# Row maxima of two heads made together on two halves of TensorE's rows, and the output projection written in half rows

## The chip, the cores and the metric

The kernel runs on one core of a Trainium2 chip. The time is the device time of one execution, in microseconds, and the figure compared is the median over runs. The engines named below are TensorE (PE, with its weight loads PEld), VectorE (DVE), ScalarE (ACT), GpSimd (POOL) and SyncE (SP), whose queue issues nearly all DMAs. Matmul results land in PSUM, which has eight banks of 128 x 512 float32.

## The reference, cut to what matters

One layer of a hybrid encoder over two sequences, 2048 and 512 tokens of width 1024. A projection feeds four groups of mixers (A to D), whose outputs are gated, put side by side and projected back. Group C is attention with 4 heads of width 64 and 2 key heads, so that two heads share their keys:

```
def one_block(q_blk):
    s = jnp.einsum("bqkgd,bskd->bkgqs", q_blk, k, preferred_element_type=jnp.float32) * scale
    p = jax.nn.softmax(s, axis=-1)
    return jnp.einsum("bkgqs,bskd->bqkgd", p.astype(v.dtype), v)
...
mix = jnp.concatenate([y_a, y_b, y_c, y_d], axis=-1)
return x + mix @ w_out
```

The softmax subtracts a row's maximum from its scores before the exponential; any number near the maximum serves, since it cancels in the quotient.

## The kernel before, in words

Tokens go in five blocks of 512: blocks 0 to 3 are the long sequence, block 4 the short one. Float32 values are carried as two float16 parts, high and low, so that products are made of two or three float16 matmuls.

The phases overlap. Phase 1 makes the columns of B and A, phase 2 makes three passes for the other columns, group B (a gated recurrence, `deltanet`) runs beside them, and `phase3` holds attention and the output projection. All instructions pass through a scheduler that writes, ahead of the run, one fixed order for each engine, by priorities and a model of the time. Attention has a priority offset of 2000000, the recurrence 3000000, the last pass of gates (lines 607 to 769) 1000000, and the output projection -2000000. On an engine the order is then fixed: what stands behind a waiting instruction waits too.

`phase3` works through a list of (sequence, block, head). One step of `attn` takes 128 keys against the block's 512 queries:

- scores `sp` (lines 909 and 910) are two matmuls: `KA` (128 rows, the keys' high part above their low part) against `qa` (the queries' high part twice), then `KB` (64 rows of the keys' high part and a row of ones) against `qb` (the queries' low part and, in its 65th row, minus the row maximum);
- `e` = exp of the scores (ACT, line 912); `p` is its high part (ACT, line 915) and its rest (line 916, DVE, at every fourth step POOL);
- twelve small matmuls add `p` times the values to `O` (line 921).

A head of blocks 0 to 3 has 16 steps, a head of block 4 has 4: 272 steps in all. The maxima for the next head come from the generator `row_max`, one unit per step: one matmul `mp` (line 884) of 128 queries against 512 keys, over all 128 rows, so high part times both key parts, and one reduction (DVE, line 886). When a head's units are through, the negated maxima are turned by four small matmuls `mr` (line 892) and put into `qb` (line 894). The first head's maxima are made ahead of all steps. `load_q` fetches a head's `qa` and `qb` (lines 870 and 871), at the start of its maxima.

Beside each step `pump` places one unit of the waiting work: first what is left of the gates (`rest`, from step 28), then the output projection of the blocks in turn (`outproj`). A unit of it is three matmuls of line 958; 24 matmuls make one group `op` of 128 tokens x 512 columns, which DVE scales and adds to `xr` (line 962) into `y`. `xr` and `y` hold whole rows of 1024. What is left when the steps are over runs behind them.

PSUM banks have the names a0, a1, b0, b1, c, d0, d1, e. `BANKS` gives a list for each use, which is gone through in turn: S for scores, M for the maxima (and for two transposes at a block's end), X for `op`. A digit behind the letter marks another list: S0 and M0 in block 0, S2 and M2 in block 4, X1 and X2 for the output projection of blocks 3 and 4.

Of the kernel before, what the change touches and what calls it, by code (L numbers as in the profile page):

```python
# [7 lines left out]
F32 = mybir.dt.float32  # L8
# [29 lines left out]
URG = 4000000  # L38
MAGIC = float(0x5F3759DF)
# [5 lines left out]
class Trunk:  # L45
    BANKS = dict(A=("a0", "a1"), B=("b0", "b1"), C=("c",), D=("d0", "d1"), E=("e",),
                 S=("a0", "a1", "b1"), O=("b0",), M=("c", "d1", "d0"), X=("e",), P=("a0", "a1", "e"),
                 AA=("a0", "a1", "d0"), F=("a0", "a1"), NA=("a0", "a1"), B0=("b0", "b1", "c", "e"), S0=("a0", "a1"), M0=("c", "b1"), X0=("e",),
                 M2=("c", "d1"), X1=("e", "d0"), X2=("e", "d0", "a0", "a1", "b1", "c"), S2=("a0", "a1", "b1"))
# [38 lines left out]
    def split3(self, parts, x, V=None):  # L88
        """x (float32, destroyed) as the sum of three float16"""
        V = V or self.nc.vector  # L90
        for i, p in enumerate(parts):
            V.tensor_copy(p, x)
            if i < 2:
                V.tensor_tensor(x, x, p, op=ALU.subtract)
# [35 lines left out]
    def mm_fm2(self, ps, w, x, mid=None):  # L130
        """two columns at once, so that each part of x is done with early"""
# [45 lines left out]
    def late_consts(self, p):  # L177
        """p: the pool of those that phase 1 alone reads"""
# [21 lines left out]
    def phase1(self):  # L200
# [3 lines left out]
        with ExitStack() as ctx:  # L204
# [31 lines left out]
            def load_x(b):  # L236
# [11 lines left out]
                if b == 0:  # L248
                    # the squares of the transposed tiles, added up over the features by the tensor engine
# [314 lines left out]
    def phase2(self, names, ep, shared, stop=None):  # L564
        """one pass over the blocks before stop for the columns in names; shared: the tags of ep for the gates.
        Returns what yields after each part of the products of a block"""
# [42 lines left out]
        def norm_sums(sq, h):  # L609
            # sq: [128, 512] squares; 1 / rms of each of the h heads, in three parts, heads on partitions  # L610
# [26 lines left out]
        def pool_block(b, f):  # L637
# [3 lines left out]
            def add(o, i, r, a, c, w):  # L641
                # o[t] = i[t - a] + i[t + c] for t in [-w, 512 + w)
# [25 lines left out]
        def pool_ready(b, f):  # L668
            """a block's part of d_x has come: what it completes"""
# [12 lines left out]
        def store_qk(dst, s):  # L682
            # s: [64 half + 32 head + j or 32 head + j, hi and lo, half, tokens]
# [9 lines left out]
        def rope_q(a, c, cs):  # L693
            # the turn leaves the norm as it is, which comes after it
# [81 lines left out]
        def chain(sq, h, finish):  # L776
            """the norm of the heads, each step in its turn"""
# [70 lines left out]
    def phase3(self, kp, ap, wp, ep, e5, rest, post):  # L848
        """SBUF pools: kp of the keys, ap of the steps, wp of the output's weights, ep and e5 of its products;
        rest: what is left of the other columns"""  # L850
        tc, nc, I = self.tc, self.nc, self.I
        V, A, G, PE, NB = nc.vector, nc.scalar, nc.gpsimd, nc.tensor, self.NB
        if True:
# [12 lines left out]
            def load_q(b, h):  # L866
                qa = ap.tile([128, 512], F16, tag="qa", name="qa")
                qb = ap.tile([65, 512], F16, tag="qb", name="qb")
# [5 lines left out]
            def row_max(seq, b, h):  # L874
                """yields after each part of the maxima of a block and head; then they stand in qb"""
                s0, n, KA, KB, vt = seq
                q = qs[b, h] = load_q(b, h)
                qa, qb = q
                nsc = n // 512
                mm = ap.tile([128, 4, nsc], F32, tag="mm", name="mm")  # L880
                for qt in range(4):
                    for sc in range(nsc):
                        mp = self.bank("M" + w0(b), [128, 512], "mp")
                        PE.matmul(mp, qa[:, qt * 128:qt * 128 + 128], KA[h // 2][:, sc * 512:sc * 512 + 512],  # L884
                                  start=True, stop=True)
# [590 lines left out]
```

## Time and profile before

| | |
|---|---|
| median of 3 runs | 1581.37 us (1578.85 to 1585.43) |
| span of the profiled execution | 1580.7 us |
| busy, PE / PEld / DVE / ACT / POOL | 1470.4 / 836.2 / 1176.9 / 815.7 / 545.7 us |
| instructions | 34819 |
| DMA | 269.66 MB, mean 171 GB/s |

The profile is one execution of the program. Its span is all that it gives as that execution's own time, and it lies 0.7 us under the median. A row of a group of instructions gives line, engine, operation, tiles out and in, shape, count, busy time, mean duration in ns, and the idle time of its engine just ahead of it with what ended it. Shapes of matmuls are rows\*columns of the array in use, then the moving operand. Matmuls overlap each other, so the busy time of PE is not a sum of durations.

### The profile page before, as it was taken

How to read it: one execution, taken by the hardware profiler on the slowest of the kernel's cores; microseconds unless marked ns; L12 is line 12 of the kernel's file. 1: busy time of each engine (PE TensorE's matmuls, PEld its weight loads, DVE VectorE, ACT ScalarE, POOL GpSimd, SP SyncE). 2: the span in 40 equal slices, each digit the busy share in tenths (PEclk: the TensorE clock that was granted, in tenths of full speed). 3: DMA queues.
4: the chain of work that ended last, by engine and by line, in shares of the span. 5: the costliest groups of instructions: out<-in, count | busy, mean ns of one | idle time of the engine just before them, and what ended most of it. 6: DMA issues, size and time to landing. Idle time of an engine off the chain costs nothing. (4 is left out here: it accounts for less than half of the span.)

```text
span 1580.7 us, 34819 instructions
## 1 busy us (share of the span) xinstructions
PE 1470.4 (93%) x13420; PEld 836.2 (53%) x13420; DVE 1176.9 (74%) x2265; ACT 815.7 (52%) x1695; POOL 545.7 (35%) x646
## 2 busy tenths in 40 slices
PE   6999999998899799999989989989899999999898
PEld 3456555543455464566545545555455555555443
DVE  6348569966969779886887768999987787786621
ACT  5245444445455755556346414566666675576500
POOL 3220220044747646344353545464222121121100
PEclk9999999998999799989899999999999999999999
DMA  8845544456565867747578897554411411413333
GB/s 252 282 167 172 187 135 124 147 192 189 159 192 194 263 180 246 209 154 214 181 225 262 286 286 241 174 175 136 161 56 60 147 37 60 164 33 124 124 127 107
DMA packets 250832, 269.66 MB, mean 171 GB/s; under 512 B 95785, under 2 KB 176681, under 8 KB 250025
## 3 DMA queue, kind: packets, MB, share of 16 engines
q1 hardware_dynamic: 250264, 267.36, 54.0%
q8 instruction: 105, 1.72, 0.5%
q14 instruction: 63, 0.51, 0.1%
q0 software_dynamic: 400, 0.07, 0.1%
HBM read 175.66 MB, written 91.77 MB: 169 GB/s over the span
## 5 line engine op out<-in xcount | busy, mean ns | idle before, releaser
L127 PEld LDWEIGHTS <-w 128*128 128x128 f16 x2280 | 222.6, 101 | 283.0 <-issue 55.7
L127 PE MATMUL accz<-xs,w 128*128 128x512 f16 x960 | 239.1, 398 | 7.9 <-DMA xs<-xs 3.9
L958 PE MATMUL op<-wo,mx 128*128 128x512 f16 x960 | 225.8, 380 | 2.6 <-DMA mx<-mix 1.9
L886 DVE TENSOR_REDUCE mm<-mp 128x1 f32<-128x512 f32 x272 | 177.5, 681 | 50.4 <-PE mp L884 49.8
L912 ACT ACTIVATE e<-sp 128x512 f32<-128x512 f32 x272 | 153.1, 597 | 89.6 <-PE sp L910 84.3
L916 POOL TENSOR_TENSOR p<-e,p 128x512 f16<-128x512 f32 x68 | 87.4, 1286 | 312.1 <-ACT p L915 262.8
L916 DVE TENSOR_TENSOR p<-e,p 128x512 f16<-128x512 f32 x204 | 171.1, 856 | 22.3 <-ACT p L915 22.2
L127 PE MATMUL acc<-xs,w 128*128 128x512 f16 x720 | 162.8, 383 | 3.8 <-POOL xs L291 1.5
L915 ACT ACTIVATE p<-e 128x512 f16<-128x512 f32 x272 | 160.7, 633 | 1.0
L921 PEld LDWEIGHTS <-p 128*128 128x128 f16 x3264 | 129.1, 97 | 56.6 <-DVE p L916 12.9
L921 PE MATMUL O<-vt,p 128*128 128x65 f16 (+1 forms) x3264 | 143.3, 193 | 9.1 <-DVE p L916 7.7
L958 PEld LDWEIGHTS <-mx 128*128 128x128 f16 x960 | 91.0, 98 | 104.5 <-DMA mx<-mix 2.0
L884 PE MATMUL mp<-ka,qa 128*128 128x512 f16 x272 | 93.3, 380 | 11.4 <-DVE mm L886 3.8
L306 DVE SCALAR_TENSOR_TENSOR cv<-raw,convw,cv 128x512 f32<-128x512 f32 x120 | 87.7, 751 | 21.2 <-POOL raw L382 20.6
L909 PE MATMUL sp<-qa,ka 128*128 128x512 f16 x272 | 102.5, 380 | 1.0 <-ACT e L912 0.6
L910 PE MATMUL sp<-qb,kb 65*128 65x512 f16 x272 | 98.3, 380 | 1.4 <-ACT qb L894 1.2
L1257 POOL TENSOR_TENSOR kd<-kv,kds 128x512 f16<-128x512 f32 x40 | 45.2, 1131 | 146.7 <-PE up L1294 120.1
L127 PE MATMUL accq<-xs,w 128*128 128x512 f16 x360 | 89.2, 394 | 3.1 <-ACT rawp L834 1.0
L400 PE MATMUL acct<-wtm,xs 128*128 128x400 f16 x480 | 85.5, 337 | 1.8 <-ACT ba L408 0.9
L291 POOL TENSOR_TENSOR xs<-xt,xs 128x512 f16<-128x512 f32 x36 | 49.1, 1387 | 75.9 <-ACT xs L288 75.6
L1131 POOL TENSOR_TENSOR at<-dt,at 128x512 f16<-128x512 f32 x40 | 53.7, 1342 | 57.3 <-ACT at L1130 47.5
L962 DVE SCALAR_TENSOR_TENSOR y<-op,xr 128x512 f32<-128x512 f32 x40 | 27.4, 685 | 55.0 <-PE op L958 54.6
(316 smaller groups left out, 2628.8 us busy)
## 6 DMA issues: line engine op xcount, KB each, us to landing
xs<-xs SPq DMA_DIRECT2D x120, 256.0 KB
kx<-kx SPq DMA_DIRECT2D x80, 256.0 KB
at<-at SPq DMA_DIRECT2D x80, 256.0 KB
tt<-tt SPq DMA_DIRECT2D x80, 256.0 KB
xt<-in_xT SPq DMA_DIRECT2D x40, 256.0 KB
xs<-xs SPq DMA_DIRECT2D x5, 2048.0 KB
kv<-kv SPq DMA_DIRECT2D x40, 256.0 KB
mix<-mixs SPq DMA_DIRECT2D x40, 256.0 KB
```

What stands on the lines that cost most here:

```text
L127: mm = self.nc.tensor.matmul(ps, w[:, a, k, :], xk, start=k + i == 0, stop=k == 7 and i == 2)
L306: V.scalar_tensor_tensor(cv, raw[:, ct, i:i + 512], self.convw[:, ct, i:i + 1], cv, op0=ALU.mult, op1=ALU.add)
L400: PE.matmul(acc[:, 0:400], xs[:, a, k, tt * 128:(tt + 1) * 128], w[:, c, k, :], start=n == 0, stop=n == 23)
L884: PE.matmul(mp, qa[:, qt * 128:qt * 128 + 128], KA[h // 2][:, sc * 512:sc * 512 + 512], start=True, stop=True)
L886: V.tensor_reduce(mm[:, qt, sc:sc + 1], mp, axis=AX.X, op=ALU.max)
L909: PE.matmul(sp, KA[kv][:, c], qa, start=True, stop=False)
L910: PE.matmul(sp, KB[kv][:, c], qb, start=False, stop=True)
L912: A.activation(e, sp, AF.Exp)
L915: A.activation(p[:, 0], e, AF.Copy)
L916: (G if st % E8 == 1 else V).tensor_tensor(p[:, 1], e, p[:, 0], op=ALU.subtract)
L921: mm = PE.matmul(O[:, qt, 0:z - a], p[:, w, q], v[:, a:z], start=st == 0 and qt == 0 and i == 0, stop=st == nst - 1 and i == 2, skip_group ...
L958: PE.matmul(op, mix[k][:, a, tt * 128:tt * 128 + 128], wo[k][:, c, n * 512:n * 512 + 512], start=i + j == 0, stop=i == 7 and j == 2)
```

## The change

- Scores get two banks instead of three in all blocks; the maxima get four (c, d1, d0, b1) in blocks 1 to 4. The output projection of block 3 gets one bank (e) instead of two.
- `row_max` now makes the maxima of heads h and h+1 together. Each unit is two matmuls of 64 rows: head h on rows 0 to 63 against `KB`, head h+1 on rows 64 to 127 against `KA`. Only high parts are multiplied. In block 0 one unit of both heads is made at a time, elsewhere two units (four matmuls), then their reductions. The generator is asked for the next part at every fourth step over the two heads, and runs to its end behind the second head.
- The four `mr` matmuls and the copy into `qb` follow for the two heads one after the other.
- `KA` has its parts the other way up, the low part above the high part.
- `qa` and `qb` have four buffers instead of two, and two heads' are loaded together.
- The output projection loads `xr` and stores `y` for 512 columns at a time, each with three buffers.

```
+MXS = 1
...
-                 S=("a0", "a1", "b1"), O=("b0",), M=("c", "d1", "d0"), X=("e",), ...
+                 S=("a0", "a1"), O=("b0",), M=("c", "d1", "d0", "b1"), X=("e",), ...
-                 M2=("c", "d1"), X1=("e", "d0"), X2=(...), S2=("a0", "a1", "b1"))
+                 M2=("c", "d1", "d0", "b1"), X1=("e",), X2=(...), S2=("a0", "a1"))
...
-                qa = ap.tile([128, 512], F16, tag="qa", name="qa")
-                qb = ap.tile([65, 512], F16, tag="qb", name="qb")
+                qa = ap.tile([128, 512], F16, tag="qa", name="qa", bufs=4)
+                qb = ap.tile([65, 512], F16, tag="qb", name="qb", bufs=4)
...
             def row_max(seq, b, h):
                 s0, n, KA, KB, vt = seq
-                q = qs[b, h] = load_q(b, h)
-                qa, qb = q
+                two = range(2)
+                for i in two:
+                    qs[b, h + i] = load_q(b, h + i)
                 nsc = n // 512
-                mm = ap.tile([128, 4, nsc], F32, tag="mm", name="mm")
-                for qt in range(4):
-                    for sc in range(nsc):
-                        mp = self.bank("M" + w0(b), [128, 512], "mp")
-                        PE.matmul(mp, qa[:, qt * 128:qt * 128 + 128], KA[h // 2][:, sc * 512:sc * 512 + 512],
-                                  start=True, stop=True)
-                        V.tensor_reduce(mm[:, qt, sc:sc + 1], mp, axis=AX.X, op=ALU.max)
+                mm = ap.tile([128, 2, 4, nsc], F32, tag="mm", name="mm")
+                rows = [slice(0, 64), slice(64, 128)]
+                keys = [KB[h // 2], KA[h // 2]]
+                units = [(qt, sc) for qt in range(4) for sc in range(nsc)]
+                at_once = 1 if b == 0 else 2
+                for j in range(0, len(units), at_once):
+                    mps = []
+                    for qt, sc in units[j:j + at_once]:
+                        for i in two:
+                            mp = self.bank("M" + w0(b), [128, 512], "mp")
+                            PE.matmul(mp, qs[b, h + i][0][rows[i], qt * 128:qt * 128 + 128],
+                                      keys[i][rows[i], sc * 512:sc * 512 + 512], start=True, stop=True)
+                            mps.append((mp, i, qt, sc))
+                    for mp, i, qt, sc in mps:
+                        V.tensor_reduce(mm[:, i, qt, sc:sc + 1], mp, axis=AX.X, op=ALU.max)
+                    if (j + at_once) % 2 == 0:
                         yield
-                m16 = ap.tile([128, 4], F16, tag="m16", name="m16")
+                m16 = ap.tile([128, 2, 4], F16, tag="m16", name="m16")
                 V.tensor_reduce(m16, mm, axis=AX.X, op=ALU.max, negate=True)
...
             def attn(seq, b, h, nxt):
...
-                    next(nxt, None)
+                    if (st + h % 2 * nst) % 4 == MXS:
+                        next(nxt, None)
...
-                for _ in nxt:
-                    pass
+                if h % 2:
+                    for _ in nxt:
+                        pass
...
             def outproj(b):
...
-                        xr = ep.tile([128, 1024], F32, tag="xr", name="xr")
-                        nc.sync.dma_start(xr, I["x"][t0:t0 + 128, :])
-                        y = ep.tile([128, 1024], F32, tag="y", name="y")
                         for n in range(2):
+                            half = slice(n * 512, n * 512 + 512)
+                            xr = ep.tile([128, 512], F32, tag="xr", name="xr", bufs=3)
+                            nc.sync.dma_start(xr, I["x"][t0:t0 + 128, half])
...
+                            y = ep.tile([128, 512], F32, tag="y", name="y", bufs=3)
+                            V.scalar_tensor_tensor(y, op, IWS / MS, xr, op0=ALU.mult, op1=ALU.add)
+                            nc.sync.dma_start(dst[:, half], y)
+                            yield
...
-                            nc.sync.dma_start(ka[hl * 64:hl * 64 + 64, c], kd[hl, kv])
+                            nc.sync.dma_start(ka[64 - hl * 64:128 - hl * 64, c], kd[hl, kv])
...
             for i, w in enumerate(work):
+                if i % 2 == 0:
+                    nxt = row_max(*work[i + 2]) if i + 2 < len(work) else iter(())
                 with tc.high_priority(offset=2000000):
-                    attn(*w, row_max(*work[i + 1]) if i + 1 < len(work) else iter(()))
+                    attn(*w, nxt)
```

More of the change, by code (lines that the diff above doesn't have):

```diff
@@ L46 @@
     BANKS = dict(A=("a0", "a1"), B=("b0", "b1"), C=("c",), D=("d0", "d1"), E=("e",),
-                 S=("a0", "a1", "b1"), O=("b0",), M=("c", "d1", "d0"), X=("e",), P=("a0", "a1", "e"),
+                 S=("a0", "a1"), O=("b0",), M=("c", "d1", "d0", "b1"), X=("e",), P=("a0", "a1", "e"),
                  AA=("a0", "a1", "d0"), F=("a0", "a1"), NA=("a0", "a1"), B0=("b0", "b1", "c", "e"), S0=("a0", "a1"), M0=("c", "b1"), X0=("e",),
-                 M2=("c", "d1"), X1=("e", "d0"), X2=("e", "d0", "a0", "a1", "b1", "c"), S2=("a0", "a1", "b1"))
+                 M2=("c", "d1", "d0", "b1"), X1=("e",), X2=("e", "d0", "a0", "a1", "b1", "c"), S2=("a0", "a1"))
     def __init__(self, tc, NP, NS, ins, outs):
@@ L887, in row_max @@
                         yield
-                m16 = ap.tile([128, 4], F16, tag="m16", name="m16")
+                m16 = ap.tile([128, 2, 4], F16, tag="m16", name="m16")
                 V.tensor_reduce(m16, mm, axis=AX.X, op=ALU.max, negate=True)
-                mr = self.bank("M" + w0(b), [128, 512], "mr")
-                for qt in range(4):
-                    PE.matmul(mr[64:65, qt * 128:qt * 128 + 128], m16[:, qt:qt + 1], self.id16,
-                              start=True, stop=True, tile_position=(0, 64))
@@ L894, in row_max @@
-                A.activation(qb[64:65, :], mr[64:65, :], AF.Copy)
+                for i in two:
+                    mr = self.bank("M" + w0(b), [128, 512], "mr")
+                    for qt in range(4):
+                        PE.matmul(mr[64:65, qt * 128:qt * 128 + 128], m16[:, i, qt:qt + 1], self.id16,
+                                  start=True, stop=True, tile_position=(0, 64))
+                    A.activation(qs[b, h + i][1][64:65, :], mr[64:65, :], AF.Copy)
             qs, ocs = {}, {}
@@ L950, in units @@
                         t0 = b * 512 + tt * 128
-                        xr = ep.tile([128, 1024], F32, tag="xr", name="xr")
-                        nc.sync.dma_start(xr, I["x"][t0:t0 + 128, :])
-                        y = ep.tile([128, 1024], F32, tag="y", name="y")
+                        dst = self.O[0][t0:t0 + 128, :] if t0 < self.NP else self.O[1][t0 - self.NP:t0 - self.NP + 128, :]
                         for n in range(2):
+                            half = slice(n * 512, n * 512 + 512)
+                            xr = ep.tile([128, 512], F32, tag="xr", name="xr", bufs=3)
+                            nc.sync.dma_start(xr, I["x"][t0:t0 + 128, half])
                             op = self.bank("X" + str(max(0, b - NB + 3)), [128, 512], "op")
@@ L957, in units @@
                                 for j, (a, c) in enumerate(((0, 0), (0, 1), (1, 0))):
-                                    PE.matmul(op, mix[k][:, a, tt * 128:tt * 128 + 128], wo[k][:, c, n * 512:n * 512 + 512],
+                                    PE.matmul(op, mix[k][:, a, tt * 128:tt * 128 + 128], wo[k][:, c, half],
                                               start=i + j == 0, stop=i == 7 and j == 2)
```

7 lines of the change are left out of this document (removed).

## The prediction

> **What bounds the kernel now.** I read the page's busy shares first, then the stages by stretches of time, because only the last third of the run holds the code that changes; then the groups of instructions of that code, its order on TensorE, and who waits for whom.
>
> ```profile
> span 1580.7 us, 34819 instructions
> PE 1470.4 (93%) x13420; PEld 836.2 (53%) x13420; DVE 1176.9 (74%) x2265; ACT 815.7 (52%) x1695; POOL 545.7 (35%) x646
> ...
> L884 PE MATMUL mp<-ka,qa 128*128 128x512 f16 x272 | 93.3, 380 | 11.4 <-DVE mm L886 3.8
> ...
> L884 PE MATMUL mp<-ka,qa x272: 376/379/586, 914.5 to 1489.1; 128*128 128x512 f16 x136
> ```
>
> The matmuls that the change pairs are the 272 of line 884, first at 914.5 us and last at 1489.1 us. By stretches (the columns are the length, busy time of PE, of the weight loads, of DVE, ACT and POOL with instruction counts, then granted clock and DMA share):
>
> ```profile
> 914.50:967.30 52.80, 44.35 (x428) 23.24 (x425) 36.55 (x70) 10.04 (x23) 23.89 (x27) 0.94 0.84 256
> 973.00:1107.00 134.00, 126.01 (x1708) 77.51 (x1705) 127.59 (x231) 85.71 (x174) 72.23 (x72) 1.00 0.54 169
> 1107.00:1140.00 33.00, 29.50 (x291) 16.10 (x288) 31.54 (x51) 21.01 (x41) 8.60 (x6) 1.00 0.56 189
> 1140.00:1500.00 360.00, 346.55 (x3655) 198.59 (x3654) 278.67 (x489) 227.02 (x426) 72.42 (x53) 1.00 0.27 88
> ```
>
> Three regimes. From 914.5 to 967 us the maxima of the first head are made, beside the recurrence and the gates, and no engine is full. From 973 to about 1140 us attention runs on block 0 and a little more beside the same work, and DVE is full (127.59 of 134, then 31.54 of 33). From 1140 to 1500 us TensorE is full (346.55 of 360) and DVE is not (278.67). After that comes a tail of output projection alone. So a TensorE saving counts in full between 1140 and 1500 us, and hardly before.
>
> Busy time is not TensorE time, since a matmul's 380 ns overlap with the next one. The tail gives the real price of a 512-column matmul: 60.02/278 = 0.216 us. That is the unit from here on (the granted clock is 1.00 in the three later stretches).
>
> ```profile
> 1516.01 60.02 PE op L958 x278
> ```
>
> **The change part by part.**
>
> *Pairs on half the rows.* The count of matmuls stays 272, each on 64 rows. A pair (head h on rows 0 to 63, head h+1 on rows 64 to 127) can stream together. The trace has no 64-row, 128-column pair, but it has the two facts needed. First, matmuls on different rows of the array do start together: on 32-row tiles, two that read different tiles start 0.01 us apart.
>
> ```profile
> 447.77 0.81 PE L127 MATMUL accq<-xs,w 128*128 128x512 f16 x3
> 448.51 0.21 PE L1201 MATMUL z1p<-d,nl 32*32 32x32 f32 x1
> 448.52 0.21 PE L1201 MATMUL z1p<-tnd,nl 32*32 32x32 f32 x1
> ```
>
> Second, the array does not go from the full shape to a part of its rows and back for nothing:
>
> ```profile
> 827.12 0.59 PE L127 MATMUL accz<-xs,w 128*128 128x512 f16 x2
> 827.65 0.39 PE L634 MATMUL rb<-rt,rexp 12*128 12x512 f16 x1
> 827.97 0.32 PE L1301 MATMUL up<-v,at 128*128 128x64 f16 x5
> ```
>
> The second of the two L127 starts at 827.12 + 0.216 = 827.34. The 12-row matmul follows 0.31 later and the next full one 0.32 after that, where two full 512-column matmuls take 0.432: an excursion costs 0.63 - 0.432 = 0.20 us. The rows at 447.77 say the same of the way in: the third L127 starts at 448.20, the first small one 0.31 later.
>
> So four maxima matmuls issued together (two units of two heads) cost 2 x 0.216 + 0.20 = 0.632 us instead of 4 x 0.216 = 0.864, a gain of 0.232. A pair by itself costs 0.416 instead of 0.432: nothing. A pair that is split by another matmul costs 2 x 0.416: 0.40 us lost. Block 0 takes its units one at a time (32 pairs of the 136): nothing gained, and DVE is the bound there. The other 104 pairs make 52 groups of four: 52 x 0.232 = -12.1 us, all in the TensorE-bound stretch or the last block. The end above is every pair split (104 x 0.40 = +42); below, pairs with no cost of the excursion (136 x 0.216 = -29.4).
>
> I take -12.1, because what would split a four is a bank that is not free, and that hardly happens. Between 1140 and 1500 us TensorE waited for a bank of the maxima five times:
>
> ```profile
> PE mp L884 <- DVE mm L886: 2.0, 5, 0.8
> PEld L921 <- DVE p L916: 5.5, 9, 1.1
> PE O L921 <- DVE p L916: 4.0, 8, 1.0
> L886 DVE TENSOR_REDUCE mm<-mp x272: 671/679/693, 914.9 to 1489.7; 128x1 f32<-128x512 f32 x136
> L910 PE MATMUL sp<-qb,kb x272: 376/379/390, 972.9 to 1500.5; 65*128 65x512 f16 x136
> ```
>
> Now there are four banks, asked for every fourth step; four reduces take 4 x 0.68 = 2.7 us, and four steps take 7.8 us (272 steps between the first and the last second score matmul, 972.9 to 1500.5 us, so 1.94 us a step).
>
> The Trainium skill bears on the size: TensorE: Matmul & The Clock Gate, Part 3, gives 3.07 times for four row tiles at 512 columns, not four times. An estimate from it (3.07/4 of 2, so 1.53 times, for a four: 0.864 - 0.563 = 0.301 us) would make this term -15.7; no run here shows it, and the sum goes by the 0.20 us of the trace.
>
> *Same work for DVE, in bursts.* 272 reduces as before, but four in a row (2.7 us) ahead of the step's p (line 916). What waits behind them is p of the following steps, and for those the O matmuls of line 921, which already waited 5.5 + 4.0 us for p. The step at which the four are made gives its own p to POOL already, which covers part. I take +2; ends -3 and +10 (twice the present wait).
>
> *Turned maxima.* The matmuls of line 892 have shape 128\*1, another excursion, once a head:
>
> ```profile
> L892 PE MATMUL mr<-id,m x80: 217/218/219, 967.3 to 1493.1; 128*1 128x128 f16 x80
> ```
>
> Twenty sets of four; now two heads' sets stand together, ten excursions fewer: up to 10 x 0.20 = -2.0. I take -1, since other work may come between.
>
> *Loads of q.* Ten load points of six DMAs in place of twenty of three.
>
> ```profile
>   DMA qa<-qs: 7.3, 7
> ...
> L870 SPq DMA_DIRECT2D qa<-qs x40: 444/515/1153, 898.3 to 1480.2; - x40
> ```
>
> These 7.3 us are TensorE idle before line 884 over the run. Each head pair is now loaded once, and in the last block (four steps a head) the next pair has eight steps to arrive instead of four. The six issues stand in one row on SP, ahead of mix and x loads, at 0.515 us each. I take -2.5; ends -7.3 and +3.
>
> *The start.* Before the first step both heads of the first pair are needed, so 32 units instead of 16: 16 x 0.68 = 10.9 us more of DVE ahead of attention. The 914.5 to 967 us row has 52.8 - 36.55 = 16 us of idle DVE to hide them, and the same 16 reduces are missing later; gates and recurrence go on meanwhile. But the next stretch is DVE-bound, so what isn't hidden is paid. I take +3; ends -3 and +10.9.
>
> *Score banks, three to two.* Block 0 already runs on two (its own list of banks), and line 909's idle for a bank over the whole run is
>
> ```profile
>   ACT e L912: 0.6, 2
> ```
>
> I take +1 (ends 0 and +3, block 0's share scaled to the 208 other steps).
>
> *Output in half rows.* Same matmuls and vector operations; twice as many loads of x and stores of y, half the size (20 more of each on SP, off the path). Of block 3, the output projection has one bank now instead of two.
>
> ```profile
> 1500.00:1580.00 80.00, 74.10 (x340) 32.78 (x337) 1.00 0.34 118
> 1576.04 0.69 DVE L962 SCALAR_TENSOR_TENSOR y<-op,xr 128x512 f32<-128x512 f32 x1 [4.49 <-PE op L958]
> 1576.76 0.34 SPq L967 DMA_DIRECT2D y_sample<-y  x1
> ```
>
> The first row is line 958 alone: 340 matmuls after 1500 us, 14 groups of 24, of which 8 are block 4's. The 6 of block 3 must each wait for the evacuation before (0.69, and by an estimate from the first and third rows 0.2 more: the matmul's own 0.38 less 0.216, and 0.03 from the vector operation's end to the next start), unless block 4's products fill the hole, which they can once their inputs are there. I take +1.5; ends 0 and +6. The last store starts at 1576.76 and the span ends 3.9 us later; half the bytes: -0.5, ends 0 and -1.5.
>
> **Sum:** -12.1 + 2 - 1 - 2.5 + 3 + 1 + 1.5 - 0.5 = -8.6 us against the profiled 1580.7: 1572.1. The median of the runs is 0.7 above that span, so 1573 us.
>
> **The rivals.**
>
> *The fours break up.* The order on TensorE is a static list made beforehand; maxima stand in it where a bank came free. For it, stretches of the present order like this one, two maxima apart by 0.65 us, about one reduce:
>
> ```profile
> 1310.40 0.38 PE L884 MATMUL mp<-ka,qa 128*128 128x512 f16 x1
> 1310.62 0.59 PE L958 MATMUL op<-wo,mx 128*128 128x512 f16 x2
> 1311.05 0.38 PE L884 MATMUL mp<-ka,qa 128*128 128x512 f16 x1
> ```
>
> Against it, the few waits for banks above. A four fully split costs +0.80 instead of -0.232, so the whole sum turns to a loss once 8.6/(52 x 1.032) = 16% of the fours are split. With a third split (17 fours): 17 x 0.80 - 35 x 0.232 = +5.5 in place of -12.1, so 1573 + 17.6 = 1591 us, slower.
>
> *The start costs what it adds.* If the first head's cadence holds (16 units between 914.5 and the first turned maxima at 967.3, though no engine was full), attention starts later and none of the 16 us of idle DVE is used: +10.9 instead of +3, 1581 us, no change. For it, DVE idle in that stretch, for a maxima matmul that stood behind others in TensorE's order:
>
> ```profile
> 948.42 0.69 DVE L886 TENSOR_REDUCE mm<-mp 128x1 f32<-128x512 f32 x1 [2.28 <-PE mp L884]
> ```
>
> Against: DVE and TensorE have other work meanwhile.
>
> *The excursion hides.* If a row-tiled group of this shape enters and leaves without the 0.20 us, the 104 pairs give 104 x 0.216 = -22.5 instead of -12.1: 1563 us. Against: every excursion I looked at in the trace pays it. The Trainium skill, TensorEngine Tiling (Array Packing), Key Properties, says that a change of tiling mode drains the engine; the trace agrees, with 0.31 us in place of 0.216.
>
> *The pairs don't run together.* Then a four costs 0.864 + 0.20: +10.4 instead of -12.1, so 1595 us. Against: the 0.01 us between starts on 32-row tiles.
>
> **How the numbers follow.** Forecast 0.48, its own range 1562 to 1584; fours break 0.20 (1591); start 0.11 (1581); hidden excursion 0.14 (1563); no concurrency 0.07 (1595). About 0.5% (8 us) is what a measurement of this kernel can tell from no change: faster is below 1573.5, slower above 1589.3. The forecast's case lies a little over half in faster (0.26), the rest in same (0.22). With the hidden excursion faster has 0.40; with the start and a quarter of the broken fours, those with few splits, same has 0.38; slower has the rest of the broken fours and no concurrency, 0.22. The range 1555 to 1594 leaves out the no-concurrency case, the heavier part of the broken fours, and a gain beyond the hidden excursion.
>
> **What would show it.** Right: matmuls of the maxima as 64\*128, starts of a pair within 0.02 us, fours in a row, about 0.63 us from the first to the next full matmul; TensorE idle before them for q below 7.3 us; first scores before about 985 us; the tail still without idle. Wrong: single maxima between scores or output products, starts within a pair 0.2 us or more apart, O waiting for p well above 5.5 + 4.0 us, scores waiting for exp, or output products waiting in the tail for the evacuation of their bank.

## The result and the profile after

The changed kernel takes 1631.76 us (median of 4 runs, 1630.59 to 1633.71) against 1583.4 us for the kernel before on the same chip: a ratio of 1.031, 95% interval 1.029 to 1.034. It is slower, where 1573 us was forecast, and outside the range. The profiled executions differ by 48.5 us (1629.2 and 1580.7).

The page of the changed kernel shows where busy time grew: TensorE has 48.2 us more with as many instructions, ScalarE 11.9 us, the others less:

```profile
span 1629.2 us, 34855 instructions
...
PE 1518.6 (93%) x13420; PEld 829.0 (51%) x13420; DVE 1166.1 (72%) x2255; ACT 827.6 (51%) x1695; POOL 541.5 (33%) x646
```

The same three regimes stand in its windows (length, busy time of PE, PEld, DVE, ACT, POOL with counts, clock, DMA share): first maxima, attention beside the other work, TensorE-bound steps.

```profile
942.40:1002.00 59.60, 53.19 (x396) 23.84 (x396) 41.33 (x79) 10.94 (x24) 22.08 (x26) 0.91 0.74 231
1002.00:1170.00 168.00, 159.73 (x1865) 88.86 (x1863) 146.63 (x260) 106.82 (x205) 71.27 (x66) 0.94 0.40 125
1170.00:1540.00 370.00, 362.27 (x3553) 185.94 (x3554) 263.33 (x462) 232.57 (x419) 64.78 (x51) 0.99 0.28 90
```

Everything begins later (first maxima 942.4 for 914.5 us), and the last stretch is as full of TensorE as before but longer. To place the loss I take marks that both kernels have, the second score matmul of given steps:

| from, to | before, us | after, us | difference |
|---|---|---|---|
| start to step 64 (end of block 0) | 1124.3 | 1147.5 | +23.2 |
| steps 64 to 256 (blocks 1 to 3) | 335.6 | 363.6 | +28.0 |
| steps 256 to 271 (block 4) | 40.6 | 30.2 | -10.4 |
| tail | 80.2 | 87.9 | +7.7 |

Blocks 1 to 3 first. The rows of the maxima (count, min/median/max ns, first and last start; under them TensorE's idle time ahead of them, in us and times):

```profile
L893 PE MATMUL mp<-kb,qa x136: 372/386/607, 942.4 to 1492.5; 64*128 64x512 f16 x136
L893 PE MATMUL mp<-ka,qa x136: 372/386/606, 942.4 to 1523.9; 64*128 64x512 f16 x136
...
  issue: 54.7, 129
```

The shape is the announced one. But 54.7 us of idle time, 129 times, stands before them with no semaphore as its end. TensorE's timeline (start, duration, operation) shows what this is:

```profile
942.44 0.39 PE L893 MATMUL mp<-kb,qa 64*128 64x512 f16 x1
942.44 0.39 PE L893 MATMUL mp<-ka,qa 64*128 64x512 f16 x1
...
1200.51 0.81 PE L974 MATMUL op<-wo,mx 128*128 128x512 f16 x3
1201.25 0.39 PE L893 MATMUL mp<-kb,qa 64*128 64x512 f16 x1
1201.57 0.60 PE L974 MATMUL op<-wo,mx 128*128 128x512 f16 x2
1202.11 0.39 PE L893 MATMUL mp<-ka,qa 64*128 64x512 f16 x1
1202.43 0.39 PE L922 MATMUL sp<-qa,ka 128*128 128x512 f16 x1
```

At 942.44 a pair runs together as foreseen. In the steady state the two halves of a pair stand apart, 0.86 us from each other, an output product between them. Of three output products the last starts at 1200.51 + 0.43 = 1200.94, the next full-array matmul at 1201.57; less one slot of 0.216 the lone 64-row matmul has cost 0.415 us. Before, a lone maxima matmul cost 0.22. Over the whole trace, 192 of the 272 stand alone, 28 times two stand together, 4 times three and only 3 times four. Counted like that (from the matmul before a run of maxima to the one behind it, less the first one's slot), the maxima take 71.0 us of TensorE after 1140 us, for 48.9 before: +22.1.

The rest of the 28 us is small. The blocks hold 14 more output products (558 for 544, 14 x 0.216 = 3.0 us), and the granted clock was 0.50 there for 10.2 us, for 3.4 before (an estimate: half of the 6.8 us more, 3.4). Block 1 alone is 20.3 us longer (110.1 to 130.4), blocks 2 and 3 are 7.7: the maxima are made further ahead, so that 73 of them stand in block 1 where 60 did, and 97 for 116 behind it.

The waits between 1140 and 1550 us (total us, times, longest) answer the rows on banks, p and exp:

```profile
PE mp L893 <- DVE mm L897: 2.1, 2, 1.7
PE O L935 <- DVE p L930: 0.6, 2, 0.5
PE sp L922 <- ACT e L925: 0.2, 1, 0.2
...
PEld L893 <- issue: 38.2, 93, 0.8
PEld L935 <- issue: 15.2, 54, 2.2
PEld L922 <- issue: 11.3, 41, 0.5
PEld L974 <- issue: 10.6, 41, 0.4
...
PEld L935 <- DVE p L930: 4.6, 10, 0.9
PEld L905 <- issue: 3.2, 10, 0.4
```

TensorE hardly waits for banks, for p or for exp. The big row is the maxima's own "issue": the entry to half the rows, paid 93 times. The three rows below it are matmuls on all rows (values, scores, output products); with the maxima on full rows, in the first experiment, two of them fall to 1.7 (scores) and 2.6 us (output products), so they are in the main the way back.

The tail's waits, from 1540 us on:

```profile
DVE y L979 <- DMA xr<-in_x: 7.7, 4, 2.8
...
PEld L974 <- DMA mx<-mix: 2.9, 1, 2.9
PE op L974 <- DVE y L979: 2.7, 3, 1.2
```

TensorE now waits here for its bank (2.7 us) and for mix (2.9 us); before, it had no idle time in the tail. VectorE, which frees the bank, waits for the half rows of x.

The start. Two windows of each kernel: from 880 us to the first step, and from there to step 64; before, then after:

```profile
880.00:972.90 92.90, 83.17 (x801) 44.81 (x800) 66.85 (x117) 22.88 (x47) 46.94 (x49) 0.96 0.88 279
972.90:1124.30 151.40, 140.81 (x1860) 86.00 (x1857) 143.43 (x260) 92.12 (x186) 75.67 (x74) 1.00 0.55 173
```

```profile
880.00:1012.50 132.50, 120.56 (x1102) 61.63 (x1099) 90.59 (x163) 31.61 (x65) 66.19 (x71) 0.96 0.81 260
1012.50:1147.50 135.00, 127.28 (x1556) 72.15 (x1552) 120.80 (x220) 85.01 (x165) 57.59 (x52) 0.92 0.37 117
```

VectorE does the same work up to step 64 (66.85 + 143.43 = 210.3 us; 90.59 + 120.80 = 211.4), so its idle time grows with the delay (34.0 to 56.1 us). The TensorE matmuls left at step 64 are the same but for the maxima. TensorE's idle time does not grow (20.3 to 19.7 us): with as many matmuls (2661 and 2658) its busy time grows by 23.9 us, which is about the delay. Two things lengthen it, and they overlap. Counted as above, the maxima (98 for 84) take about 47 us for 30, waits for banks included. And the granted clock was 0.50 for 30.7 us of that time, for 6.8 before; an estimate from this is up to 12 us, half of the difference. Neither is thereby shown to be the cause.

### The profile page after: what moved, and what is told of

Read it like the earlier page. It is cut to its first block, busy times and chain, and to the rows that moved or that the text cites. A ratio compares the mean times of both kernels' runs of the same rounds, so it can differ in the third digit from the quotient of the medians.

```text
span 1629.2 us, 34855 instructions
## 1 busy us (share of the span) xinstructions
PE 1518.6 (93%) x13420; PEld 829.0 (51%) x13420; DVE 1166.1 (72%) x2255; ACT 827.6 (51%) x1695; POOL 541.5 (33%) x646
## 4 chain that ended last, share of the span: by engine, by line
PE 51%; DVE 22%; DMA 14%; issue 5%; ACT 4%; SPq 2%; POOL 2%; DVEq 0%; ACTq 0%; POOLq 0%
PE op L974 11%; PE accz L128 6%; PE O L935 6%; PE acc L128 4%; PE mp L893 4%; PE sp L922 3%; DVE cv L307 3%; PE sp L923 3%; DVE ltmp L1168 2%; PE accq L128 2%; PE accu L128 2%; DMA xs<-xs 2%; DVE mm L897 2%; PE acct L401 1%; DMA mx<-mix 1%
## 5 line engine op out<-in xcount | busy, mean ns | idle before, releaser
L974 PE MATMUL op<-wo,mx 128*128 128x512 f16 x960 | 231.8, 384 | 9.7 <-DMA mx<-mix 7.0
L897 DVE TENSOR_REDUCE mm<-mp 128x1 f32<-128x512 f32 x272 | 181.6, 683 | 65.2 <-PE mp L893 64.7
L930 POOL TENSOR_TENSOR p<-e,p 128x512 f16<-128x512 f32 x68 | 83.6, 1229 | 358.3 <-ACT p L929 289.4
L930 DVE TENSOR_TENSOR p<-e,p 128x512 f16<-128x512 f32 x204 | 158.8, 792 | 33.5 <-ACT p L929 33.0
L935 PE MATMUL O<-vt,p 128*128 128x65 f16 (+1 forms) x3264 | 149.1, 195 | 2.0 <-DVE p L930 1.6
L923 PE MATMUL sp<-qb,kb 65*128 65x512 f16 x272 | 104.9, 389 | 0.0
L401 PEld LDWEIGHTS <-xs 128*128 128x128 f16 x480 | 46.9, 98 | 35.5 <-issue 2.2
```

The lines of the kernel that those rows point to most:

```text
L401: PE.matmul(acc[:, 0:400], xs[:, a, k, tt * 128:(tt + 1) * 128], w[:, c, k, :], start=n == 0, stop=n == 23)
L897: V.tensor_reduce(mm[:, i, qt, sc:sc + 1], mp, axis=AX.X, op=ALU.max)
L923: PE.matmul(sp, KB[kv][:, c], qb, start=False, stop=True)
L930: (G if st % E8 == 1 else V).tensor_tensor(p[:, 1], e, p[:, 0], op=ALU.subtract)
L935: mm = PE.matmul(O[:, qt, 0:z - a], p[:, w, q], v[:, a:z], start=st == 0 and qt == 0 and i == 0, stop=st == nst - 1 and i == 2, skip_group ...
L974: PE.matmul(op, mix[k][:, a, tt * 128:tt * 128 + 128], wo[k][:, c, half], start=i + j == 0, stop=i == 7 and j == 2)
```

## Experiments

The letters in the expectations are theories. S: a 64-row matmul that stands apart pays the way to half the rows and back, and this is the loss of blocks 1 to 3. T: the late first step is what costs. Q: the order of the loads makes it late. H: the second head's maxima ahead of the first step do. B: the banks and the bursts of four. D: VectorE's additional work ahead of block 1. The others are spelled out in place. "Step 64" is the mark of the table above.

**Full rows again, the rest as changed.** High parts times both key parts, so the maxima of the kernel before, in the new loop.

```
-  PE.matmul(mp, qs[b, h + i][0][rows[i], ...], keys[i][rows[i], ...], ...)
+  PE.matmul(mp, qs[b, h + i][0][:, ...], KA[h // 2][:, ...], ...)
```

> The changed kernel with each matmul of the maxima on all 128 rows again (high part against both key parts, as before the change), so the array's shape never changes for them; pairing, banks, steps and loads stay as changed. Theory S (excursions): 192 of the 272 matmuls stand alone in TensorE's list and each costs 0.415 us instead of 0.216; taking the excursion away brings the lone ones back to 0.216 and the time to 1595 to 1612 us (at least the 22 us that the maxima cost more after 1140 us). Rival T (late start): attention still starts 40 us late, so the time stays above 1620. Rival B (banks, one output bank, half rows): above 1620 as well.

1605.79 us, ratio to before 1.0119 [1.0082, 1.0156]: 26 us faster than the changed kernel. Blocks 1 to 3 in one window, before, after and here (second column the length):

```profile
1124.30:1459.90 335.60, 326.77 (x3484) 187.56 (x3484) 265.41 (x456) 220.28 (x414) 70.06 (x52) 0.99 0.26 87
```

```profile
1147.50:1511.10 363.60, 356.95 (x3496) 181.66 (x3495) 267.25 (x461) 233.37 (x421) 67.83 (x53) 0.99 0.27 87
```

```profile
1146.90:1486.10 339.20, 327.72 (x3498) 187.65 (x3496) 265.44 (x461) 233.41 (x421) 69.63 (x53) 1.00 0.30 94
```

24.4 of the 28 us are gone with the 64 rows. The loss of the start is not: step 64 stands at 1146.9. From 880 to 1147 us TensorE is idle for 29.6 us in this kernel, and its clock was 0.50 for 17.1 us.

**Parts held together.** The first matmul of a part waits for the last reduction of the part before, and the others are issued straight behind it.

```
+  if mpi is None:
+      mpi = PE.matmul(*mm_args, start=True, stop=True).ins     # waits for lastred
+  else:
+      with tc.high_priority(offset=8000000), tc.issue_after(mpi):
+          mpi = PE.matmul(*mm_args, start=True, stop=True).ins
```

> The changed kernel with the matmuls of one part of the maxima held together in TensorE's list: the first waits for the last reduction of the part before, the others follow it at once. The list then has 43 fours, 35 twos and 16 alone in place of 3, 28 and 192. Theory S: a four costs 0.632 us, a pair 0.416; the maxima cost TensorE some 55 to 60 us instead of 115, and the time falls to 1595 to 1605 us. Rival T: attention still starts at about 1010 us and the time stays above 1620. Rival P (pairs do not run at once on this shape): a four costs 1.06 us and the time stays above 1620.

1606.71 us, 1.0133 [1.0108, 1.0158], 25 us faster than the changed kernel and just outside the range of theory S. In TensorE's order 16 maxima stand alone now, and 43 times four stand together:

```profile
1202.06 0.38 PE L933 MATMUL sp<-qb,kb 65*128 65x512 f16 x1
1202.38 0.39 PE L897 MATMUL mp<-kb,qa 64*128 64x512 f16 x1
1202.38 0.39 PE L903 MATMUL mp<-ka,qa 64*128 64x512 f16 x1
1202.60 0.38 PE L903 MATMUL mp<-kb,qa 64*128 64x512 f16 x1
1202.61 0.38 PE L903 MATMUL mp<-ka,qa 64*128 64x512 f16 x1
1202.91 0.39 PE L932 MATMUL sp<-qa,ka 128*128 128x512 f16 x1
```

0.85 us from the last full matmul to the next, less its slot: 0.634 for the four. The starts of a pair lie 0.003 to 0.004 us apart. So the pairs run together, and a held four costs what was forecast (0.632). Yet it ends no earlier than the kernel with full rows. Over blocks 1 to 3 its maxima take about 33 us by the same count, for 50 there, but the blocks need 336.3 us for 339.2. Part of the other 14 us shows as a clock of 0.50 for 9.4 us, where the kernel with full rows had none (an estimate: 4.7 us), and as longer waits for mix (first row: held parts; second: full rows, between 1147 and 1486 us). The rest is not accounted for.

```profile
PEld L984 <- DMA mx<-mix: 8.8, 3, 3.7
```

```profile
PEld L974 <- DMA mx<-mix: 6.4, 4, 2.2
```

**64 rows put into the kernel before,** singly, nothing paired or moved. Only high parts are multiplied.

```
-  PE.matmul(mp, qa[:, ...], KA[h // 2][:, ...], ...)
+  PE.matmul(mp, qa[0:64, ...], KB[h // 2][0:64, ...], ...)
```

> The kernel before, with one edit: each maxima matmul uses 64 rows, the queries' high part against the keys' high part, one head at a time, one unit a step as before. So only high parts are multiplied, as in the changed kernel, but nothing is paired and no bank, load or reduce moves. Theory S (each change to 64 rows and back costs 0.20 us of TensorE): its 272 maxima stand in 223 runs in the order, so 223 x 0.20 = 45 us of TensorE, of which about 70% fall after step 64, where TensorE is full: step 64 at the same time within 5 us, steps 64 to 256 longer by 25 to 32 us, end +25 to +32 (ratio 1.016 to 1.020). Rival B (the excursion costs only beside the bursts of four and their banks): within 5 us of the kernel before.

1620.15 us, 1.024 [1.021, 1.0269], or 38 us: more than expected, and B falls. Blocks 1 to 3:

```profile
1132.90:1496.80 363.90, 357.32 (x3483) 180.70 (x3483) 266.35 (x457) 222.66 (x414) 68.57 (x52) 0.99 0.24 81
```

+28.3 us, as in the changed kernel, for about 28 us more of TensorE for the maxima. The other 15 us of its profiled execution lie in block 0 (8.6, where at most 5 was expected), block 4 (3.6) and the tail (2.9, which is 14 more output products). For blocks 1 to 3, S is shown from both sides.

**Two parts of the change alone on the kernel before.** The banks of the changed kernel, and the output in half rows (the lines of the change's diff).

> The kernel before, with the banks of the changed kernel alone (two for scores, four for the maxima, one for the output projection of block 3). If the banks cost what the tail shows: 4 to 8 us slower than before, all of it in the tail. If two score banks hold the steps up too: 10 us or more, spread over blocks 1 to 4. If a fourth bank for the maxima helps: no slower than before.

> The kernel before, with the output handled in half rows alone (three buffers of 512 columns each for x and y). Expected: within 5 us of the kernel before; the prediction priced it at -0.5 us at the end. If the doubled loads and stores stand in the way of q and mix loads on SP: 5 us or more slower, with longer waits of TensorE for DMAs.

Banks: 1588.23 us, 1.003 [1.0005, 1.0056]; in its profile the tail is 88.3 us for 80.2, and step 64 comes 7.7 us earlier. Half rows: 1581.85 us, 0.998 [0.996, 1.001], no difference that can be told. Neither delays the start (step 64 at 1116.6 and 1121.5).

**The keys loaded early,** in the changed kernel and in the one with held parts.

```
+  with tc.high_priority(offset=2000000):
       seq = load_kv(s0, n)
```

> The changed kernel with the loads of keys and values given the priority of attention, so that they are issued ahead of the gates' loads; 185 of the maxima's matmuls still stand alone. Theory T (late start): the first maxima come some 25 us earlier, the first step before 990 us, and the time falls by 15 to 25 us, to 1607 to 1617. Theory S: the time stays within 8 us of 1632, since what the excursions cost is untouched and the start was filled with gates.

> Both of the above: the parts of the maxima held together (45 fours, 32 twos, 19 alone) and the keys loaded early. If S and T both hold and add up: 1575 to 1590 us. If only S: as the grouped kernel alone, 1595 to 1605. If only T: 1607 to 1617.

1625.14 us, 1.0253 [1.0224, 1.0282], and 1599.12 us, 1.0085 [1.0055, 1.0116]. The first step came at 973 and 981 us, 39 and 38 us earlier, and the end only 7 and 8 us. T's 15 to 25 us were not there. Step 64 came 15 us earlier in each, but 93 and 63 matmuls of the gates were then still to do. And 46 and 58 us ahead of the first step ran at half clock (last section), so these two runs don't settle what a late first step costs.

**Block 0 singly.** Held parts, but in block 0 one head at a time on full rows; the first pair, for block 1, is made beside heads 2 and 3.

```
-  for _ in row_max(*work[0]):
+  for _ in row_max1(*work[0]):       # the single-head loop of the kernel before
...
-      nxt = row_max(*work[i + 2]) if i + 2 < len(work) else iter(())
+      nxt = row_max(*work[i + 2]) if 0 < i < len(work) - 2 else iter(())
...
-      attn(*w, nxt)
+      attn(*w, nxt, row_max1(*work[i + 1]) if i < 3 else ())
```

> The grouped kernel, with block 0 as before the change: its heads one at a time on all rows, 16 units ahead of the first step instead of 32, then one unit a step; the first pair (block 1) is made beside heads 2 and 3 of block 0. Theory T2 (two heads ahead of the first step hold TensorE and DVE up; the grouped kernel passes step 64 at 1149.5 us, 25 us after the kernel before): the first step comes 15 us earlier or more, step 64 by 1140, and the time falls by 10 to 18 us, to 1589 to 1597. Rival D (DVE has 10.9 us more to do before block 1 in either order): the first step comes earlier but step 64 and the time stay within 5 us of the grouped kernel's 1606.

1607.73 us, 1.0154 [1.013, 1.0177]: the first step is 38 us earlier than with held parts, step 64 only 5 us (1144.8), the end not at all. The trace shows where it went. Between heads 2 and 3 of block 0 no step runs from 1083.1 to 1120.5 us, 37.4 us (9.8 before, from 1077.6 us), while 31 maxima matmuls are made one after the other, beside their reductions, most of the time at half clock (length, busy PE, PEld, DVE, ACT, POOL, clock):

```profile
1093.90:1124.60 30.70, 19.69 (x78) 5.24 (x78) 25.93 (x55) 4.46 (x9) 3.92 (x3) 0.50 0.22 73
```

So this kernel pays at another place, and doesn't tell what two heads ahead of the first step cost.

**Two banks again for block 3's output,** three for block 4's maxima, one unit at a time there; held parts.

```
-  M2=("c", "d1", "d0", "b1"), X1=("e",)
+  M2=("c", "d1", "b1"), X1=("e", "d0")
-  at_once = 1 if b == 0 else 2
+  at_once = 1 if b in (0, NB - 1) else 2
```

> The grouped kernel, with two banks again for the output projection of block 3 (and three for the maxima of block 4, made one unit at a time). Theory X (one bank leaves holes in the tail): the time from the last step to the end falls from 84.5 us to about 80, the kernel by 3 to 5 us, to 1601 to 1604. Rival: the tail is longer only because a few more output products are left for it, then it stays within 2 us.

1596.79 us, 1.0079 [1.0059, 1.01], 10 us faster than held parts alone, more than expected. The tail is 83.4 us for 84.5, within the 2 us of the rival. But it holds 14 more output products (357 for 343, 3.0 us) and none of the 2.7 us for which TensorE waited for the bank, so the bank has the part that theory X gave it. And 9 of the 10 us are there at step 64 already, ahead of all use of these banks. The order is worked out anew for each edit, and the start moves with it; so a difference of some 9 us at the start between two of these kernels can come from the order alone.

**VectorE's load at the start.** On the kernel before, 16 reductions of block 0 twice; on the kernel before and on the last one, more of p on GpSimd in block 0.

```
+  if (b, h) == (0, 2):
+      V.tensor_reduce(mm2[:, qt, sc:sc + 1], mp, axis=AX.X, op=ALU.max)
```

```
-  (G if st % E8 == 1 else V).tensor_tensor(...)
+  (G if st % (2 if b == 0 else E8) == 1 else V).tensor_tensor(...)
```

> The kernel before, and the 16 reduces of one head in block 0 (head 2, made beside the steps of head 1) are made twice, the second time into a tile that nobody reads: 16 x 0.68 = 10.9 us more of VectorE in the stretch where it is full, as much as the changed kernel adds there by being a pair of heads ahead. Theory D (that is what the changed kernels pay before step 64): step 64 about 11 us later, end +8 to +11 (ratio 1.005 to 1.007). Rival N (VectorE's share is small; the order and TensorE's idle time make the loss): step 64 and end within 4 us of the kernel before.

> The kernel before with every second, not every fourth, rest of p in block 0 made on GpSimd: 16 x 0.68 = 10.9 us less for VectorE and 16 x 1.16 = 18.6 us more for GpSimd, which is idle for 62 of 134 us there. Theory D: step 64 up to 11 us earlier and the end -6 to -11 (ratio 0.993 to 0.996). Rival N: within 4 us, or a little slower, since p then waits 0.48 us longer at 16 steps.

> The kernel with parts held together and two banks for the output projection of block 3, with the same edit in block 0 (every second rest of p on GpSimd). Theory D: step 64 8 to 11 us earlier (1129 to 1132 against 1140) and the end at 1584 to 1587. Rival N: step 64 within 4 us, end 1591 to 1598.

1.0005 [0.9987, 1.0022]; 1.0054 [1.003, 1.0078]; 1.0162 [1.0135, 1.0189]. D is borne out by none of the three: 10.9 us more for VectorE moved step 64 by 5.5 us, half of what D asked for, and nothing was left of that at the end; 10.9 us less made both kernels slower. In these two p also waits longer for GpSimd, so they are the weaker tests.

**The order of the loads.** The SP queue of the changed kernel, then of the kernel before (start, duration, line):

```profile
911.98 1.89 SPq L742 DMA_DIRECT2D xs<-xs  x3
...
932.49 0.88 SPq L1016 DMA_DIRECT2D ka<-ks  x1
```

```profile
907.61 0.45 SPq L1003 DMA_DIRECT2D ka<-ks  x1
...
912.12 0.57 SPq L741 DMA_DIRECT2D xs<-xs  x1
```

Four buffers of q let the loads of four heads go ahead, and behind these the keys' loads fall behind the gates' loads of xs. Four kernels around this: four buffers (and KA the other way up) on the kernel with half rows; the same with each head's maxima one head further ahead, singly on full rows; the kernel with two output banks where later loads of q wait for a step's scores; and that with pairs only from block 2 on.

```
-  qa = ap.tile([128, 512], F16, tag="qa", name="qa")                # four buffers
+  qa = ap.tile([128, 512], F16, tag="qa", name="qa", bufs=4)
...
-  attn(*w, row_max(*work[i + 1]) if i + 1 < len(work) ...)          # one head ahead
+  attn(*w, row_max(*work[i + 2]) if i + 2 < len(work) ...)
...
+  for d in ds[:3 if lastsp else 0]:                                 # q waits for scores
+      tc.add_manual_dep(d.ins, lastsp[0].name, ...)
...
-  nxt = row_max(*work[i + 2]) if 0 < i < len(work) - 2 else ...     # pairs late
+  nxt = row_max(*work[i + 2]) if 4 < i < len(work) - 2 else ...
```

> The kernel before with output in half rows (alone that gave 0.998), and qa and qb in four buffers (KA the other way up, too): no maxima are paired or moved. The loads of q of two more heads now stand ahead of the keys' loads on SP, which fall behind nine loads of xs for the gates. Theory Q (this order of loads is what delays the start): first keys' load and first maxima 20 to 28 us later, first step at 990 to 1000 us, step 64 at 1132 to 1142 (1121.5 without it), end +10 to +18 (ratio 1.005 to 1.010). Theory H (the second head's maxima ahead of the first step are what costs): within 4 us of the kernel with half rows alone.

> As the kernel with four buffers of q, and each head's maxima, still made singly on all rows, one head further ahead: two heads' maxima before the first step. Theory Q: step 64 within 6 us of the kernel with four buffers alone. Theory H: 10 to 15 us later than that, at the end too (ratio 1.012 to 1.018 against before).

> The kernel with parts held together and two banks for block 3's output, with one edit: a load of q, but for the first two heads', waits for the scores of the step it belongs to, so that it cannot be issued ahead of the keys' loads. SP's order ahead of attention is then that of the kernel before. Theory Q: first maxima at about 915, first step at 975 to 985, step 64 at 1120 to 1128, end at 1576 to 1582, a little faster than before. Theory H: step 64 at 1134 to 1140, end at 1590 to 1596.

> Blocks 0 and 1 as in the kernel before (one head at a time, full rows), pairs in held parts from block 2 on, loads of q waiting as above, two banks for block 3's output. In the order 26 fours stand together. Theory S (the fours pay where they hold) with a start that costs nothing: step 64 at 1118 to 1126, step 128 as before's 1234, then 4 to 6 us saved over blocks 2 and 3; end 1573 to 1580 (ratio 0.994 to 0.998). Rival (grouping holds up the steps by as much as it saves): end at 1584 to 1590.

1.0022 [0.9999, 1.0044]; 1.0002 [0.9974, 1.0029]; 1.0096 [1.0061, 1.0132]; 1.0094 [1.0061, 1.0127]. With four buffers the first maxima do come at 945.1 us and the first step at 980.7 (910.2 and 968.5 with half rows alone), but step 64 only 8 us later, at 1129.3, and the end 0.4% later than 0.998: Q has a small part at most. The second kernel doesn't do what it was made for: its order keeps the second head's maxima behind the first step (18 maxima matmuls stand ahead of that step, as with four buffers alone, where the changed kernel has 32). And where the loads of q wait, the first maxima start at 924.7 us but the first step still at 1010.6, with 32 maxima ahead of it, and step 64 comes at 1154.8, later than both theories said. Q falls as the cause of the 23 us; H is left without a clean test.

In the kernel with late pairs the start is whole (step 64 at 1127.2). Its two windows are block 1, then blocks 2 and 3; below them the same of the kernel with half rows alone:

```profile
1127.20:1257.10 129.90, 119.21 (x1195) 64.37 (x1194) 100.25 (x176) 77.33 (x140) 22.72 (x18) 0.97 0.24 79
1257.10:1478.20 221.10, 214.12 (x2341) 117.33 (x2339) 169.55 (x302) 154.09 (x281) 43.87 (x35) 1.00 0.31 99
```

```profile
1121.50:1231.70 110.20, 107.43 (x1162) 61.72 (x1162) 87.54 (x150) 72.94 (x137) 25.66 (x18) 1.00 0.23 73
1231.70:1455.80 224.10, 218.10 (x2309) 125.03 (x2307) 173.44 (x302) 147.02 (x277) 42.34 (x34) 1.00 0.29 94
```

Blocks 2 and 3, behind the change to pairs, are 3.0 us shorter. That isn't shown to be the fours: the changed kernel with full rows, which can gain nothing by them, needed 222.4 us for these steps. The block in which the first pair is made beside single heads is 19.7 us longer: TensorE is busy 11.8 us more (33 more matmuls, a clock of 0.97 for 1.00) and idle 7.9 us more, and VectorE works 12.7 us more. So a loss like that of the start stands where the first pair is made.

**The 16 additional maxima spread evenly** over block 1, in the last kernel.

```
-  next(one, None)
+  credit[0] += 1.3          # units a step, out of three single heads and the first pair
+  while credit[0] > 0:
+      credit[0] -= next(one, 99)
```

> The kernel with pairs from block 2 on, with one edit: in block 1 the maxima (three single heads and the first pair, 80 matmuls) are asked for evenly, 1.3 a step, in place of one a step and, beside the last 32 steps, four more at every fourth. Theory C (the crowding of 48 reduces into 32 steps makes that block long): steps 64 to 128 take 114 to 118 us in place of 129.8, the rest stays, end at 1578 to 1584 (ratio 0.996 to 1.000). Rival R (the extra maxima cost that wherever they lie, or the single and paired maxima disturb each other's banks): 125 to 132 us, end within 5 us of the kernel with late pairs, 1590 to 1598.

1597.32 us, 1.0093 [1.0061, 1.0125]; block 1 took 124.2 us for 129.9, far from C's 114 to 118, and the later blocks gave the 5 us back. C falls. Why the first pair costs some 20 us where it is made, in block 0 or in block 1, stays open. None of these kernels is shown to beat the kernel before.

## Why the prediction was wrong, point by point

**The fours (-12.1): the step that failed.** "What would split a four is a bank that is not free, and that hardly happens": the second half held, the first did not. Between 1170 and 1540 us stand 158 maxima matmuls of the changed kernel. The four banks go in turn, so each takes the bank of the fourth one before it (turned maxima and transposes shift this now and then). 139 of the 158 start more than 3 us after that one's reduction has ended, only 5 less than 1 us after it. The banks were free, and the order, made beforehand, put scores and output products between the four all the same: 3 fours stand in the trace. By what rule it did so no run shows; tied together in the list, 43 stand. The rival that the fours break up had the outcome, with a chance of 0.20; its reason, that maxima stand where a bank came free, isn't what the trace shows, and it was priced with a third of the fours split. The end above, every pair split at +42 us, was priced on the right side: measured were +22.1 us of TensorE after 1140 us and +28 us of time in blocks 1 to 3.

The prices themselves held: 0.415 us for a lone 64-row matmul (forecast 0.416), 0.634 for a four (0.632), starts 0.004 us apart. So two rivals fall: that the excursion hides, and that the pairs don't run together. The Trainium skill's factor in TensorE: Matmul & The Clock Gate, Part 3, from which 0.563 us was estimated for a four, is not what these pairs give: they take 0.634 us, as the trace's 0.20 us had it.

**The start (+3, ends -3 and +10.9): mis-sized, by a mechanism that was not seen.** +23.2 us at step 64. The forecast and its rival both counted VectorE's 10.9 us, and as much work given to VectorE alone, on the kernel before, left nothing at the end. TensorE's busy time grew there by 23.9 us, with 30.7 us at half clock for 6.8: the prediction read the granted clock of the kernel before and put no term for a change of it. The late loads of the keys (6 more DMAs of q ahead of them, which the prediction counted at 0.515 us each and not by what they are moved past) are a small part. What sets off the loss stays open.

**VectorE in bursts (+2).** TensorE waits for p 0.6 + 4.6 us between 1140 and 1550 us; it was 4.0 + 5.5 between 1140 and 1500 us. No loss, within the ends.

**Turned maxima (-1).** The entry to that shape shows ten times ("L905 <- issue", 3.2 us), once for two heads: as forecast, though what it saved cannot be told from the rest.

**Loads of q (-2.5, ends -7.3 and +3).** No wait for qa is left among those of line 893, and block 4 runs 10.4 us shorter. Only part of that can be the loads: 22 of its output products (57 for 79, 22 x 0.216 = 4.8 us) run elsewhere, 14 in blocks 1 to 3 and 8 in the tail (1.7 us), and 4 maxima matmuls stand in it for 12.

**Score banks (+1).** 0.2 us of waits for exp: nothing, as the end below said.

**Output (+1.5 for the bank, -0.5 for the last store).** Half rows alone: 0.998, which can't be told from no change. In the tail the one bank cost 2.7 us and mix 2.9, the 8 further products 1.7. That was within the end of 6 for the bank; that VectorE would wait for half rows of x (7.7 us) while it holds the bank was not said.

## What to carry to other kernels

A matmul on half the array's rows pays about 0.2 us when it stands alone between full ones, so a pair of 512 columns wins nothing and two pairs win 0.23 us, and only if the order holds them together. In an order made beforehand, matmuls that are asked for together need not stand together, even where their banks are free: look at what the order does with them before counting on it. Tying them held most of the fours here, but of some 17 us that the maxima took less than on full rows in blocks 1 to 3, only 3 arrived in the time.

## What the runs showed of the hardware that was not expected

TensorE ran at half clock for long stretches in the two kernels with early keys, while its rows are busy for most of the time (length, busy PE, PEld, DVE, ACT, POOL, then the clock, 0.50). The first row is the changed kernel with early keys, the second the one with held parts, the third a stretch of the changed kernel itself.

```profile
930.60:975.00 44.40, 37.06 (x373) 21.88 (x370) 39.89 (x80) 8.45 (x21) 25.00 (x30) 0.50 0.73 223
```

```profile
922.70:980.70 58.00, 36.30 (x452) 25.81 (x452) 47.40 (x93) 10.99 (x27) 34.54 (x41) 0.50 0.80 246
```

```profile
1040.70:1054.40 13.70, 13.70 (x123) 7.34 (x121) 11.40 (x23) 8.61 (x17) 1.83 (x3) 0.50 0.22 71
```

It is no fault of the record: in the first of them a maxima matmul lasts 0.58 us there, for the 0.39 shown above.

```profile
945.83 0.58 PE L893 MATMUL mp<-ka,qa 64*128 64x512 f16 x1
```

In the two kernels with early keys, the recurrence's small matmuls and the first maxima stood there with gaps between them; in the third row the records leave no gap. The Trainium skill, TensorE: Matmul & The Clock Gate, Part 1, has the full clock come back after about 3.4 us of sustained work; the trace shows that 63% to 83% by the records, with gaps, did not bring it back for 44 and 58 us. From 880 us to step 64 the clock was 0.50 for 3 to 14 us in the kernels that make no two heads' maxima together before step 64, and for 14 to 65 us in the nine that do. What an early first step won, a slow TensorE gave back in part, by how much no run tells.
